# Two-part matrix products in mixers A and C: one wide product for the high weight part, its two sums joined on eviction

## The chip, the cores and the metric

One NeuronCore of a Trainium2 chip runs the whole program. The metric is the device time of one execution in microseconds; the median of several executions counts, and less is better. The profile is of one more execution of the same program.

## The reference

A trunk of four pre-RMSNorm residual layers over x (1, 256 tokens, 2048 features), float32, with mixers A, B, C, A and a final RMSNorm. Each layer does `x = x + mixer(rmsnorm(x))`.

- A is dilated sliding-window attention. `proj = h @ w_in` gives q, k and v of three groups (windows 128, 512, 2048 with dilations 1, 4, 16) with 8 heads of 128, and a gate of 1024 columns. q and k get a rotary on their first 32 dims; scores are scaled by 128^-0.5; the three groups' outputs are joined by a softmax over their log denominators; the result is multiplied by `silu(gate)` and goes through `w_out`.
- B is a convolution module: `val * sigmoid(glu)`, a depthwise convolution of 31 taps, LayerNorm, SiLU, a gate, and `w_out`.
- C is a retention in two chunks of 128 tokens with 8 heads (q, k of 256 dims with rotary, v of 512), a normalisation per head, `silu(gate)` and `w_out`.

Nearly all of the arithmetic lies in the products with the weight matrices, 391 MB of them, each read once.

## The kernel before, in words

x is held transposed: eight tiles `X[c]` of [128 features, 2, 256 tokens], and beside them `XHL[c]`, [128, 2, 2, 256], the normalised input in a high and a low part (L297, L303), so that a product of float32 quality is made of fp32r products: high weight by high x, high weight by low x, low weight by high x. The RMSNorm's per-token factor `rstd` is put in only when a result leaves PSUM.

Weights come as slabs of 1 MB, called pieces (`chunk_ws`, `chunk_xs`, `group_ws` list them all in order). The main loop (L1062) takes piece i: its products `p.mm`, then `cut(i + 2)`, which splits a later slab into `wh` (ScalarE copy, L1056) and `wl` (VectorE subtract, L1057; for some pieces of B on GpSimd) and issues the load of the slab after on SP (L1045); then `after`, the eviction of a finished chunk; then `pop`, which takes steps from the list `side` by their costs and a budget. A step pushed with `brk=True` ends that pop, and steps pushed by `after` wait for the next piece, since `avail` is counted before. `raw`, `wh` and `wl` have three buffers each. PSUM has 4 accumulator banks (`ps_acc`), 2 for scores (`ps_s`) and 2 for transposes (`ps_t`).

Three forms of products stand in the code. `mm_ws` (L138) keeps 128 weight columns in the array and streams 256 tokens: per k tile and 128 features the three products L154, L155 and L156, all into one half of a bank, so that a chunk of 256 features is one bank. A slab of 8 k tiles and 256 columns has 48 such products. `mm_xs` (L176) keeps x in the array and streams 512 weight columns (L188 to L190, 24 products a slab). `mm_xs2` (L159) does the same with 256 columns and is used in B alone.

In A (L354) six `chunk_xs` chunks give v; then, for each of four head pairs, six `chunk_ws` chunks of two slabs give q and k of the three groups. `after_qk` (L471) multiplies the bank by `rstd_p` (L475), shuffles 32 partitions (L477) and rotates them on GpSimd (L478 to L480). The last k of a head pair calls `attention(hp)` (L483), which pushes seven groups (L541), each of one step of `scores` (L488), `turn` and `values` for the four units of a head pair; the exponent is `A.activation(p, p, AF.Exp, bias=..., scale=128^-0.5)` (L504). Then four gate chunks follow (`after_gate`, L543), whose step `z` (L548) builds the input of the output projection, and in layer 0 eight output chunks of one slab each (L592), which `new_x` (L287) adds to X. In layer 3 the output projection is of the form `mm_xs`.

C (L885) has for each of eight heads a q and a k chunk of the form `mm_ws` (`after_qk`, L896: two multiplies from the bank, L902 and L903, and two adds), and v and gate chunks of the form `mm_xs`. After every second head an output projection over a quarter of the features runs, 8 chunks of one slab each, 32 in all (`outp`, L1008, with `new_x`).

`ScalarE` runs its instructions in the order in which they are issued, as do VectorE, GpSimd and the SP queue; the order above is thus each engine's own.

Of the kernel before, what the change touches and what calls it, by code (L numbers as in the profile page):

```python
# [54 lines left out]
def tile_hybrid_trunk(ctx: ExitStack, tc, x, positions, norm_w, final_norm_w, a_w_in, a_w_out,  # L55
# [82 lines left out]
    def mm_ws(np_, p, kts, hold, xs, nb=1):  # L138
# [18 lines left out]
        return f  # L157

    def mm_xs2(np_, p, kts, hold, xs):  # L159

        def f(wh, wl):
            if p == 0:
                hold["ps"] = [ps_acc()]
            kk = len(kts)
            for t in range(2):
                for i in range(kk):
                    ps = hold["ps"][0][:, t * 256:(t + 1) * 256]
                    xh, xl = (v[:, t * 128:(t + 1) * 128] for v in xs(kts[i]))
                    T.matmul(ps, xh, wh[:, i, :], start=p == 0 and t == 0 and i == 0, stop=False,  # L169
                             skip_group_check=True)  # L170
                    T.matmul(ps, xh, wl[:, i, :], start=False, stop=False, skip_group_check=True)  # L171
                    T.matmul(ps, xl, wh[:, i, :], start=False, stop=p == np_ - 1 and i == kk - 1,  # L172
                             skip_group_check=True)
        return f

    def mm_xs(np_, p, kts, hold, xs):  # L176

        def f(wh, wl):
            if p == 0:
                hold["ps"] = [ps_acc(), ps_acc()]  # L180
            kk = len(kts)
            order = [(i, t) for i in range(kk) for t in range(2)]
            if p == np_ - 1:
                order = [(i, t) for t in range(2) for i in range(kk)]
            for i, t in order:
                ps = hold["ps"][t]
                xh, xl = (v[:, t * 128:(t + 1) * 128] for v in xs(kts[i]))
                T.matmul(ps, xh, wh[:, i, :], start=p == 0 and i == 0, stop=False)  # L188
                T.matmul(ps, xh, wl[:, i, :], start=False, stop=False)  # L189
                T.matmul(ps, xl, wh[:, i, :], start=False, stop=p == np_ - 1 and i == kk - 1)  # L190
        return f

    def x_of(kt):
        return XHL[kt // 2][:, kt % 2, 0], XHL[kt // 2][:, kt % 2, 1]

# [5 lines left out]
    def chunk_ws(w, c0, nk, after, xs=x_of, kt0=0, before=None, lo=lambda p: "v", budget=3.0, hold=None,  # L201
                 mm=None):
        hold = {} if hold is None else hold
        mm = mm or mm_ws
        np_ = nk // 8
        for p in range(np_):
            kts = list(range(p * 8, p * 8 + 8))
            pieces.append(Piece(wslab(w, kt0 + p * 8, 8, c0, 256), 8, 256, mm(np_, p, kts, hold, xs),
                                after=(lambda: after(hold["ps"][0])) if p == np_ - 1 else None,
                                before=before if p == 0 else None, lo=lo(p), budget=budget))  # L210
# [76 lines left out]
    def new_x(c, ps, layer, perm):  # L287

        V.tensor_tensor(X[c], v3(ps), X[c], op=OP.add)
        if layer is None:  # L290
# [63 lines left out]
    def layer_a(L, wi, wo, first, next_layer, final):  # L354
# [116 lines left out]
        def after_qk(g, w, hp):  # L471
            def f(ps):
                q = lt([128, 2, S], F32, "qk", 8)
                QK[g, w, hp] = q
                V.tensor_tensor(q, v3(ps), row2(rstd_p), op=OP.mult)  # L475
                sw = tmp([128, 2, S])[:32]
# [6 lines left out]
        def attention(hp):  # L483
            units = [(h, qt) for h in range(2) for qt in range(2)]
            U = {}
            scale = 128.0 ** -0.5

            def scores(u):  # L488
# [6 lines left out]
                for g in (1, 2):  # L495
# [6 lines left out]
                                       stt[:, 0:1])  # L502
                V.tensor_scalar(stt[:, 1:2], stt[:, 0:1], -scale, None, op0=OP.mult)
                A.activation(p, p, AF.Exp, bias=stt[:, 1:2], scale=scale, accum_out=stt[:, 2:3])  # L504
                V.reciprocal(stt[:, 3:4], stt[:, 2:3])
# [12 lines left out]
            def values(u):  # L518
# [12 lines left out]
                A.activation(o[:, h, qt * 128:(qt + 1) * 128], ps, AF.Copy)  # L531

            for n in range(7):
                def group(n=n):
                    if n >= 3:
                        values(units[n - 3])
                    if 2 <= n < 6:
                        turn(units[n - 2])
                    if n < 4:
                        scores(units[n])  # L540
                push(2.9, group, brk=True)  # L541

        def after_gate(hp):  # L543
            def f(ps):
                g = lt([128, 2, S], F32, "g", 3)
                V.tensor_tensor(g, v3(ps), row2(rstd_p), op=OP.mult)

# [13 lines left out]

        s1, s2 = norm_stats(True, True)

# [23 lines left out]
        def z_of(kt):  # L587
            return ZT[kt // 2][:, kt % 2, 0], ZT[kt // 2][:, kt % 2, 1]

# [70 lines left out]
    def layer_b(L, wi, wo, next_layer):  # L660
# [4 lines left out]
        def tok(ps, t):  # L665
            return ps[t] if isinstance(ps, list) else ps[:, t * 256:(t + 1) * 256]

# [217 lines left out]
    def layer_c(L, wi, wo, next_layer):  # L885
# [10 lines left out]
        def after_qk(h, w):  # L896
            def f(ps):
# [3 lines left out]
                m2 = tmp([128, 2, S])  # L901
                V.tensor_tensor(m1, v3(ps), st["rope"][:, 0:1].to_broadcast([128, 2, S]), op=OP.mult)  # L902
                V.tensor_tensor(m2, v3(ps), st["rope"][:, 1:2].to_broadcast([128, 2, S]), op=OP.mult)  # L903
                V.tensor_tensor(o[:, 0], m1[:, 0], m2[:, 1], op=OP.subtract)
# [103 lines left out]
        def outp(p):  # L1008
            def z_of(kt):
                z = ZT[4 * p + kt // 2]  # L1010
                return z[:, kt % 2, 0], z[:, kt % 2, 1]
            need = 4 * p + 3
# [128 lines left out]
```

## Time and profile before

| | us |
|---|---|
| median of 3 executions | 2270.89 |
| lowest and highest | 2269.66 to 2271.91 |
| the profiled execution | 2272.37 |
| its span, first to last instruction | 2270.6 |
| mean granted TensorE clock | 0.991 |

The profiled execution's time is 1.8 us longer than its span. The profile has a page with the busy time of each engine, the chain of work that ended last and groups of instructions by line, and a trace that answers what each engine did when. PE is TensorE's matrix products, PEld its weight loads, DVE is VectorE, ACT ScalarE, POOL GpSimd and SP the queue that issues the loads. A product's duration in the trace runs through the array's pipeline, so that products overlap; the distance from one start to the next is what one costs.

### The profile page before, as it was taken

How to read it: one execution, taken by the hardware profiler on the slowest of the kernel's cores; microseconds unless marked ns; L12 is line 12 of the kernel's file. 1: busy time of each engine (PE TensorE's matmuls, PEld its weight loads, DVE VectorE, ACT ScalarE, POOL GpSimd, SP SyncE). 2: the span in 40 equal slices, each digit the busy share in tenths (PEclk: the TensorE clock that was granted, in tenths of full speed). 3: DMA queues.
4: the chain of work that ended last, by engine and by line, in shares of the span. 5: the costliest groups of instructions: out<-in, count | busy, mean ns of one | idle time of the engine just before them, and what ended most of it. 6: DMA issues, size and time to landing. Idle time of an engine off the chain costs nothing.

```text
span 2270.6 us, 34549 instructions
## 1 busy us (share of the span) xinstructions
PE 2227.4 (98%) x15024; PEld 2066.4 (91%) x15024; DVE 1333.5 (59%) x1537; ACT 976.0 (43%) x905; POOL 554.4 (24%) x273
## 2 busy tenths in 40 slices
PE   8999999999999997999999999999999999999998
PEld 7789999999998877989889889899988889999996
DVE  5545565556597886565555545455556446555554
ACT  4343433445444444444443444344355333333353
POOL 3005334321478972100000000000001015334311
PEclk9999999999999998999999999999999999999999
DMA  6555445446555553555555555555555555444444
GB/s 222 186 199 176 159 158 169 152 141 197 170 179 189 174 167 134 184 188 180 179 186 177 201 168 174 196 175 170 191 173 171 190 191 182 151 164 167 154 145 148
DMA packets 301424, 395.95 MB, mean 174 GB/s; under 512 B 6615, under 2 KB 212823, under 8 KB 301269
## 3 DMA queue, kind: packets, MB, share of 16 engines
q1 hardware_dynamic: 299280, 391.14, 51.9%
q8 instruction: 117, 1.92, 0.3%
q10 hardware_dynamic: 1592, 1.93, 0.3%
q0 software_dynamic: 400, 0.67, 0.1%
q14 instruction: 35, 0.28, 0.0%
HBM read 391.63 MB, written 2.10 MB: 173 GB/s over the span
## 4 chain that ended last, share of the span: by engine, by line
PE 92%; DVE 3%; POOL 2%; ACT 2%; issue 1%; DMA 0%; DVEq 0%; ACTq 0%
PE ps_acc L156 16%; PE ps_acc L155 16%; PE ps_acc L154 16%; PE ps_acc L189 11%; PE ps_acc L188 11%; PE ps_acc L190 11%; PE ps_acc L172 1%; PE ps_acc L171 1%; PE ps_acc L169 1%; PE ps_t L530 1%; POOL tmp L479 1%; DVE wl L1057 1%; PE ps_t L965 1%; PE ps_s L497 1%; ACT wh L1056 1%
## 5 line engine op out<-in xcount | busy, mean ns | idle before, releaser
L1057 DVE TENSOR_TENSOR wl<-raw,wh 128x2048 fp32r<-128x2048 f32 (+1 forms) x329 | 782.2, 2379 | 559.3 <-ACT wh L1056 557.2
L1056 ACT ACTIVATE wh<-raw 128x2048 fp32r<-128x2048 f32 (+1 forms) x371 | 703.4, 1898 | 713.3 <-PE ps_acc L155 333.9
L154 PE MATMUL ps_acc<-xhl,wh 128*128 128x256 f32 x2304 | 657.6, 285 | 0.0
L156 PE MATMUL ps_acc<-xhl,wl 128*128 128x256 f32 x2304 | 652.7, 283 | 0.0
L155 PE MATMUL ps_acc<-xhl,wh 128*128 128x256 f32 x2304 | 652.6, 283 | 0.1
L189 PE MATMUL ps_acc<-wl,xhl 128*128 128x512 f32 x1152 | 451.1, 392 | 3.0 <-DVE wl L1057 2.8
L188 PE MATMUL ps_acc<-wh,xhl 128*128 128x512 f32 x1152 | 453.8, 394 | 0.2 <-ACT wh L1056 0.2
L190 PE MATMUL ps_acc<-wh,xhl 128*128 128x512 f32 x1152 | 450.6, 391 | 0.0
L155 PEld LDWEIGHTS ps_acc<-xhl,wh 128*128 128x128 f32 x2304 | 442.5, 192 | 0.7 <-DVE xhl L303 0.3
L154 PEld LDWEIGHTS ps_acc<-xhl,wh 128*128 128x128 f32 x2304 | 442.5, 192 | 0.4
L156 PEld LDWEIGHTS ps_acc<-xhl,wl 128*128 128x128 f32 x2304 | 442.3, 192 | 0.0
L189 PEld LDWEIGHTS ps_acc<-wl,xhl 128*128 128x128 f32 x1152 | 217.7, 189 | 48.4 <-DVE wl L1057 4.4
L190 PEld LDWEIGHTS ps_acc<-wh,xhl 128*128 128x128 f32 x1152 | 217.4, 189 | 45.4
L188 PEld LDWEIGHTS ps_acc<-wh,xhl 128*128 128x128 f32 x1152 | 217.7, 189 | 44.9 <-ACT wh L1056 0.6
L478 POOL TENSOR_TENSOR qk<-qk,ropeA 32x512 f32<-32x512 f32 x48 | 63.6, 1325 | 611.6 <-DVE tmp L477 611.6
L1057 POOL TENSOR_TENSOR wl<-raw,wh 128x2048 fp32r<-128x2048 f32 x42 | 194.6, 4635 | 69.7 <-ACT wh L1056 54.2
L274 POOL COPY ssq<-tmp 128x512 f32<-128x512 f32 x4 | 5.6, 1411 | 830.0 <-ACT tmp L299 812.0
L154 PE MATMUL ps_acc<-z,wh 128*128 128x256 f32 x512 | 145.5, 284 | 0.0
L156 PE MATMUL ps_acc<-z,wl 128*128 128x256 f32 x512 | 145.2, 284 | 0.0
L155 PE MATMUL ps_acc<-z,wh 128*128 128x256 f32 x512 | 144.7, 283 | 0.0
L479 POOL TENSOR_TENSOR tmp<-tmp,ropeA 32x512 f32<-32x512 f32 x48 | 121.0, 2520 | 0.0
L722 DVE SCALAR_TENSOR_TENSOR ps_s<-u,bw,ps_s 128x256 f32<-128x256 f32 x232 | 91.8, 483 | 26.2 <-ACT ps_s L720 26.2
(224 smaller groups left out, 2610.5 us busy)
## 6 DMA issues: line engine op xcount, KB each, us to landing
raw<-in_a_w_in_dram SPq DMA_DIRECT2D x159, 1024.0 KB, 5.0
raw<-in_c_w_in_dram SPq DMA_DIRECT2D x96, 1024.0 KB, 5.0
raw<-in_b_w_in_dram SPq DMA_DIRECT2D x48, 1024.0 KB, 5.1
raw<-in_c_w_out_dram SPq DMA_DIRECT2D x32, 1024.0 KB, 5.7
raw<-in_a_w_out_dram SPq DMA_DIRECT2D x16, 1024.0 KB, 5.7
raw<-in_b_w_out_dram SPq DMA_DIRECT2D x16, 1024.0 KB, 5.0
xin<-in_x_dram SPq DMA_DIRECT2D x4, 512.0 KB, 8.7
out_dram<-qk SPq DMA_DIRECT2D x8, 256.0 KB, 2.6
```

Of the source, the lines that this page charges most:

```text
L154: T.matmul(ps, w_h, xh, start=st, stop=False, skip_group_check=True)
L155: T.matmul(ps, w_h, xl, start=False, stop=False, skip_group_check=True)
L156: T.matmul(ps, w_l, xh, start=False, stop=last and i == kk - 1, skip_group_check=True)
L169: T.matmul(ps, xh, wh[:, i, :], start=p == 0 and t == 0 and i == 0, stop=False, skip_group_check=True)
L188: T.matmul(ps, xh, wh[:, i, :], start=p == 0 and i == 0, stop=False)
L189: T.matmul(ps, xh, wl[:, i, :], start=False, stop=False)
L190: T.matmul(ps, xl, wh[:, i, :], start=False, stop=p == np_ - 1 and i == kk - 1)
L478: G.tensor_tensor(q[:32], q[:32], ropeA[:, 0:1].to_broadcast([32, 2, S]), op=OP.mult)
L479: G.tensor_tensor(sw, sw, ropeA[:, 1:2].to_broadcast([32, 2, S]), op=OP.mult)
L722: V.scalar_tensor_tensor(ct[:, j] if k == TAPS - 1 else acc[j], src, w, acc[j], op0=OP.mult, op1=OP.add)
L1056: A.activation(wh[:, sl], r[:, sl], AF.Copy)
L1057: (V if p.lo == "v" else G).tensor_tensor(wl[:, sl], r[:, sl], wh[:, sl].bitcast(F32), op=OP.subtract)
```

## The change

`chunk_ws` takes a new form of products, `mm_wj`, for A and C: a chunk has two banks, one per 128 features. The high weight part meets the high and the low part of x, which lie side by side in `XHL` (and in the `z` tiles), in one product of 512 columns; the low weight part meets the high x in one of 256 columns. The bank then holds two sums, which are joined on eviction: `joined` copies the second to SBUF on ScalarE and adds the first on VectorE, per bank; `new_x` adds both to X, one after the other. In A, q is no longer multiplied by `rstd_p`; the factor goes into the scale of the exponent, per query row (`qs_`, two small instructions behind the column form of rstd). An empty step with `brk=True` is pushed ahead of attention's seven groups. B keeps its forms; `mm_xs` and `mm_xs2` only fetch the two parts of x in another way.

```diff
+    def mm_wj(np_, p, kts, hold, xs):
+        def f(wh, wl):
+            if p == 0:
+                hold["ps"] = [ps_acc(), ps_acc()]
+            last = p == np_ - 1
+            kk = len(kts)
+            order = [(nt, i) for nt in range(2) for i in range(kk)]
+            if hold.get("kouter") and p == 0:
+                order = [(nt, i) for i in range(kk) for nt in range(2)]
+            for nt, i in order:
+                x2 = xs(kts[i])
+                ps = hold["ps"][nt]
+                w_h = wh[:, i, nt * 128:(nt + 1) * 128]
+                w_l = wl[:, i, nt * 128:(nt + 1) * 128]
+                T.matmul(ps, w_h, x2, start=p == 0 and i == 0, stop=False, skip_group_check=True)
+                T.matmul(ps[:, 0:S], w_l, x2[:, 0], start=False, stop=last and i == kk - 1,
+                         skip_group_check=True)
+        return f
+
+    def sums(ps):
+        return [(b[:, 0:S], b[:, S:2 * S]) for b in ps]
+
+    def joined(dst, ps):
+        for j, (a, b) in enumerate(sums(ps)):
+            A.activation(dst[:, j], b, AF.Copy)
+            V.tensor_tensor(dst[:, j], a, dst[:, j], op=OP.add)
...
     def x_of(kt):
-        return XHL[kt // 2][:, kt % 2, 0], XHL[kt // 2][:, kt % 2, 1]
+        return XHL[kt // 2][:, kt % 2]
...
     def chunk_ws(w, c0, nk, after, xs=x_of, kt0=0, before=None, lo=lambda p: "v", budget=3.0, hold=None,
...
-        mm = mm or mm_ws
+        mm = mm or mm_wj
...
-                                after=(lambda: after(hold["ps"][0])) if p == np_ - 1 else None,
+                                after=(lambda: after(hold["ps"])) if p == np_ - 1 else None,
...
     def new_x(c, ps, layer, perm):
-        V.tensor_tensor(X[c], v3(ps), X[c], op=OP.add)
+        if isinstance(ps, list):
+            for h in range(2):
+                for j, parts in enumerate(sums(ps)):
+                    V.tensor_tensor(X[c][:, j], parts[h], X[c][:, j], op=OP.add)
+        else:
+            V.tensor_tensor(X[c], v3(ps), X[c], op=OP.add)
...
                 QK[g, w, hp] = q
-                V.tensor_tensor(q, v3(ps), row2(rstd_p), op=OP.mult)
+                joined(q, ps)
+                if w == 1:
+                    V.tensor_tensor(q, q, row2(rstd_p), op=OP.mult)
...
-                V.tensor_scalar(stt[:, 1:2], stt[:, 0:1], -scale, None, op0=OP.mult)
-                A.activation(p, p, AF.Exp, bias=stt[:, 1:2], scale=scale, accum_out=stt[:, 2:3])
+                V.tensor_scalar(stt[:, 1:2], stt[:, 0:1], qs_[:, 2 + qt:3 + qt], None, op0=OP.mult)
+                A.activation(p, p, AF.Exp, bias=stt[:, 1:2], scale=qs_[:, qt:qt + 1], accum_out=stt[:, 2:3])
...
+            push(0.0, lambda: None, brk=True)
             for n in range(7):
                 def group(n=n):
...
         def after_gate(hp):
             def f(ps):
                 g = lt([128, 2, S], F32, "g", 3)
-                V.tensor_tensor(g, v3(ps), row2(rstd_p), op=OP.mult)
+                joined(g, ps)
+                V.tensor_tensor(g, g, row2(rstd_p), op=OP.mult)
...
+        def s2():
+            s2_()
+            qs_ = st["qs"] = lt([128, 4], F32, "qs")
+            V.tensor_scalar(qs_[:, 0:2], rcol, 128.0 ** -0.5, None, op0=OP.mult)
+            V.tensor_scalar(qs_[:, 2:4], rcol, -(128.0 ** -0.5), None, op0=OP.mult)
...
-                V.tensor_tensor(m1, v3(ps), st["rope"][:, 0:1].to_broadcast([128, 2, S]), op=OP.mult)
-                V.tensor_tensor(m2, v3(ps), st["rope"][:, 1:2].to_broadcast([128, 2, S]), op=OP.mult)
+                joined(m1, ps)
+                V.tensor_tensor(m2, m1, st["rope"][:, 1:2].to_broadcast([128, 2, S]), op=OP.mult)
+                V.tensor_tensor(m1, m1, st["rope"][:, 0:1].to_broadcast([128, 2, S]), op=OP.mult)
```

## Rows read from the trace of the kernel before

**Rows 1.** The page, busy us (share of the span) xinstructions of each engine.

```profile
PE 2227.4 (98%) x15024; PEld 2066.4 (91%) x15024; DVE 1333.5 (59%) x1537; ACT 976.0 (43%) x905; POOL 554.4 (24%) x273
```

**Rows 2.** The page, the chain that ended last, by engine.

```profile
PE 92%; DVE 3%; POOL 2%; ACT 2%; issue 1%; DMA 0%; DVEq 0%; ACTq 0%
```

**Rows 3.** Groups by form: out<-in, shapes xcount | busy us, mean ns | idle before.

```profile
L154 PE MATMUL ps_acc<-xhl,wh 128*128 128x256 f32 x2304 | 657.6, 285 | 0.0
...
L154 PE MATMUL ps_acc<-z,wh 128*128 128x256 f32 x512 | 145.5, 284 | 0.0
...
L154 PE MATMUL ps_acc<-v,wh 128*128 128x256 f32 x128 | 36.3, 283 | 0.0
```

**Rows 4.** Timeline of PE (start us, us), 256-column products, 18 steps apart.

```profile
399.81 0.28 PE L155 MATMUL ps_acc<-xhl,wh 128*128 128x256 f32 x1
...
401.97 0.28 PE L155 MATMUL ps_acc<-xhl,wh 128*128 128x256 f32 x1
```

**Rows 5.** Timeline of PE, 512-column products, 14 steps apart.

```profile
149.69 0.39 PE L190 MATMUL ps_acc<-wh,xhl 128*128 128x512 f32 x1
...
152.86 0.39 PE L189 MATMUL ps_acc<-wl,xhl 128*128 128x512 f32 x1
```

**Rows 6.** Stretches of 100 us: busy by engine, then granted clock, DMA share, GB/s.

```profile
100.00:200.00 100.00, 100.00 (x591) 89.32 (x591) 49.80 (x31) 36.56 (x21) 13.28 (x8) 1.00 0.57 190
...
400.00:500.00 100.00, 98.88 (x820) 98.32 (x820) 58.31 (x70) 41.43 (x41) 31.30 (x18) 1.00 0.45 148
```

**Rows 7.** Timeline of PE, a 256-column product followed by a 512-column one.

```profile
989.23 0.28 PE L156 MATMUL ps_acc<-xhl,wl 128*128 128x256 f32 x1
989.35 0.40 PE L188 MATMUL ps_acc<-wh,xhl 128*128 128x512 f32 x1
```

**Rows 8.** Timeline of PE, a 512-column product followed by a 256-column one.

```profile
161.93 0.39 PE L190 MATMUL ps_acc<-wh,xhl 128*128 128x512 f32 x1
162.15 0.28 PE L154 MATMUL ps_acc<-xhl,wh 128*128 128x256 f32 x1
```

**Rows 9.** Timeline of PE, first scores of a head pair, slab behind.

```profile
237.03 0.60 PE L494 MATMUL ps_s<-qk 128*128 128x256 f32 x2
...
239.22 0.36 PE L154 MATMUL ps_acc<-xhl,wh 128*128 128x256 f32 x1
```

**Rows 10.** Timeline of PE, second scores of that head pair, slab behind.

```profile
245.05 0.60 PE L494 MATMUL ps_s<-qk 128*128 128x256 f32 x2
...
245.84 0.36 PE L154 MATMUL ps_acc<-xhl,wh 128*128 128x256 f32 x1
```

**Rows 11.** Waits of PE: line <- releaser: us in total, times, longest.

```profile
PE ps_s L497 <- POOL qk L480: 9.0, 8, 1.1
```

**Rows 12.** Timeline of all engines, eviction and rotary of the last k.

```profile
231.47 0.69 DVE L475 TENSOR_TENSOR qk<-ps_acc,rstd_p 128x512 f32<-128x512 f32 x1 [1.64 <-PE ps_acc L156]
...
234.27 3.32 POOL L479 TENSOR_TENSOR tmp<-tmp,ropeA 32x512 f32<-32x512 f32 x1
...
237.66 1.25 POOL L480 TENSOR_TENSOR qk<-qk,tmp 32x512 f32<-32x512 f32 x1
```

**Rows 13.** Groups by form: VectorE and ScalarE reading 256 columns of a bank.

```profile
L617 DVE TENSOR_TENSOR qk<-ps_acc,x 128x256 f32<-128x256 f32 x16 | 5.9, 418 | 8.4 <-PE ps_acc L190 8.4
...
L680 ACT ACTIVATE sg<-ps_acc,rcol 128x256 f32<-128x256 f32 x8 | 3.4, 470 | 13.5 <-PE ps_acc L172 11.0 <-DVE rcol L269 2.6
```

**Rows 14.** Timeline of DVE, a residual add in C's output projection [idle before].

```profile
1689.84 0.69 DVE L289 TENSOR_TENSOR x<-ps_acc,x 128x512 f32<-128x512 f32 x1 [1.59 <-PE ps_acc L156]
```

**Rows 15.** Timeline of all engines, start of layer 0's output projection.

```profile
528.81 0.69 DVE L558 TENSOR_TENSOR v<-tmp,v 128x512 fp32r<-128x512 f32 x1 [0.70 <-ACT v L557]
...
529.85 0.28 PE L155 MATMUL ps_acc<-v,wh 128*128 128x256 f32 x1
```

**Rows 16.** DMA issues: KB each, median us to landing.

```profile
raw<-in_a_w_in_dram SPq DMA_DIRECT2D x159, 1024.0 KB, 5.0
```

More of the change, by code (lines that the diff above doesn't have):

```diff
@@ L167, in f @@
                     ps = hold["ps"][0][:, t * 256:(t + 1) * 256]
-                    xh, xl = (v[:, t * 128:(t + 1) * 128] for v in xs(kts[i]))
+                    xh, xl = (xs(kts[i])[:, h, t * 128:(t + 1) * 128] for h in range(2))
                     T.matmul(ps, xh, wh[:, i, :], start=p == 0 and t == 0 and i == 0, stop=False,
@@ L186, in f @@
                 ps = hold["ps"][t]
-                xh, xl = (v[:, t * 128:(t + 1) * 128] for v in xs(kts[i]))
+                xh, xl = (xs(kts[i])[:, h, t * 128:(t + 1) * 128] for h in range(2))
                 T.matmul(ps, xh, wh[:, i, :], start=p == 0 and i == 0, stop=False)
@@ L485, in attention @@
             U = {}
-            scale = 128.0 ** -0.5
+            qs_ = st["qs"]
             def scores(u):
@@ L560, in after_gate @@
             return f
-        s1, s2 = norm_stats(True, True)
+        s1, s2_ = norm_stats(True, True)
+        def s2():
[3 more added lines that the diff above has]
+            V.tensor_scalar(qs_[:, 2:4], rcol, -(128.0 ** -0.5), None, op0=OP.mult)
         n0 = len(pieces)
@@ L587, in z_of @@
         def z_of(kt):
-            return ZT[kt // 2][:, kt % 2, 0], ZT[kt // 2][:, kt % 2, 1]
+            return ZT[kt // 2][:, kt % 2]
         if not final:
@@ L665, in tok @@
         def tok(ps, t):
-            return ps[t] if isinstance(ps, list) else ps[:, t * 256:(t + 1) * 256]
+            return ps[t] if len(ps) == 2 else ps[0][:, t * 256:(t + 1) * 256]
         def turn(src, dst, bank=ps_acc):
@@ L1010, in z_of @@
                 z = ZT[4 * p + kt // 2]
-                return z[:, kt % 2, 0], z[:, kt % 2, 1]
+                return z[:, kt % 2]
             need = 4 * p + 3
```

## The prediction

> **What bounds the kernel now.** I read first the busy shares of the engines. The reader sees TensorE (PE) busy for 98% of the span and VectorE (DVE) for 59% [rows 1]. Then the chain of work that ended last: 92% of it is PE [rows 2]. So PE's products set the time, and a change pays by what it takes off PE's own line, or loses by what it makes PE wait for.
>
> Next the groups by form, to count the products that the change touches. The three products of `mm_ws` (L154 to L156) run 2304 times each against `xhl` (the input projections of mixers A and C), 512 times against `z` (C's output projection) and 128 against `v` (the output projection of layer 0's A) [rows 3]. B's output projection, against `big`, keeps `mm_ws`. So 2304 + 512 + 128 = 2944 triples become pairs.
>
> The busy time of these rows is no price: 284 to 285 ns each includes a pipeline that overlaps. The price is the distance from start to start, in the timeline. For 256 columns, 18 steps take 401.97 - 399.81 = 2.16 us: 0.120 us each [rows 4]. For 512 columns, 14 steps take 152.86 - 149.69 = 3.17 us: 0.2264 us each [rows 5]. The granted clock is 1.00 in the windows around both [rows 6], that is 2.4 GHz, at which 256 columns stream in 0.1067 us and 512 in 0.2133 us. So each product costs its columns and about 0.0133 us more, at either width. That fixed part is what the change can save.
>
> **The change, part by part.**
>
> Products. A triple of 256 columns costs 3 x 0.120 = 0.360 us. The pair has the same 768 columns in two products: 0.2266 + 0.120 = 0.3466 us, taking 0.0133 over the columns for the wide one. Each pair so saves 0.0133 us; 2944 x 0.0133 = 39.2 us. A mixed sequence does not stand in the trace, but its two steps do: a 256-column product followed by a 512-column one starts it 0.12 us later [rows 7], and a 512-column one followed by a 256-column one 0.22 us later [rows 8]. Neither order pays a surcharge, and neither gives more than the steady pace. From the steady rows the bounds are 2944 x 0.0124 = 36.5 us (0.2276 for the wide product, a nanosecond above) and 2944 x 0.0136 = 40.0 us (0.2264).
>
> On the same point the Trainium skill, "TensorE: Matmul & The Clock Gate", section "Back-to-back issue gap", gives a warm gap of N/2.4 + 2.5 ns. By it a triple would be 327.5 ns, a pair 325.0 ns, and the saving 2944 x 2.5 ns = 7.4 us (an estimate from that page); the rows show 13.3 ns, not 2.5, and the rows decide.
>
> Attention one slab later. Before, the first scores of each head pair came one slab behind the last k projection and waited for its rotary part on GpSimd (POOL). From the first product of the scores to the next slab's first product took 239.22 - 237.03 = 2.19 us [rows 9]; the second group of the same four products took 245.84 - 245.05 = 0.79 us [rows 10]. So 1.40 us is lost per head pair. The list of waits has it 8 times, four head pairs in two layers [rows 11]: 8 x 1.40 = 11.2 us. Is it gone? k is taken off at 231.47 and POOL ends it at 237.66 + 1.25 = 238.91 [rows 12]: 7.4 us. The new eviction is longer: ScalarE (ACT) copies 0.47 [rows 13], then the second copy and two adds of 0.42, of which one hides beside the copy, and the 0.69 multiply: 0.47 + 0.42 + 0.42 + 0.69 = 2.0 us in place of 0.69, so 1.3 us more, 8.7 us in all. Two slabs are now 2 x 16 x 0.3466 = 11.1 us. 2.4 us are left, so I take all 11.2 off. The bounds are 11.2 and 0.
>
> The empty step pushed ahead of attention issues nothing on any engine, so every queue (SP's loads, POOL's rotary work, DVE, ACT) only sees the seven groups behind one more slab's split. What is queued behind the scores on PE is the next slab, which no longer stands still. Scaling q in the exponent instead of in the eviction drops 24 multiplies on DVE, off the chain; the two small scale columns per layer are 4 tiny instructions. I cost both at nothing, under cover of DVE's 41% of idle time; without the cover the multiplies' loss would be a gain, and the four, at most 0.42 us each, would cost 1.7 us.
>
> Evictions. A bank now holds the high and low sums side by side. Each chunk of q, k or gate adds two ACT copies (0.47 each) and replaces one DVE operation by two of 0.42 and up to two more. It lies beside the next slab's products, since four accumulator banks hold two chunks. In the output projections the residual add becomes four of 0.42 = 1.67 us, in place of 0.69: 1.0 us more. In the steady slab there DVE idles 1.59 us [rows 14] of every 48 x 0.120 = 5.76 us; the slab shrinks to 5.55, so 1.59 - 1.0 - 0.2 = 0.4 us stays idle. Hidden, but nearly used up. If it were not, the price is the overrun per slab: at 0.69 an add (the whole-bank price, upper bound) 2.76 - 0.69 = 2.07 us more, 0.7 us over per slab, 40 such slabs, 28 us. I take nothing, since the 0.42 row has the same shape and the same kind of operands.
>
> Loads. A slab of 1 MB lands 5.0 us after its issue at the median [rows 16]; it must come every 5.55 us, three are in flight, and the 512-column stretches already run a slab in 24 x 0.2266 = 5.44 us. No cost.
>
> Start of layer 0's output projection. The last gate's z now meets both x parts in the first product. The seventh k tile comes 36 products after the start, 36 x 0.120 = 4.3 us; before, the low part was done at 528.81 + 0.69 = 529.50, and its first reader started at 529.85 [rows 15]. The eviction adds 1.3 us, the pairs bring the reader 0.2 us + 0.12 us forward, and the last attention group in front pushes it back by some 0.5 us: 0.35 - 1.3 - 0.3 + 0.5 = a stall of 0.8 us, once. Layer 3 needs that tile a slab later and pays nothing. Bounds: 0 and 2 us.
>
> Sum. The profiled execution took 2272.37 us, 1.5 above the median of the runs shown. 2272.4 - 39.2 - 11.2 + 0.8 = 2222.8; less that 1.5, and rounded up a little for small waits: **2222 us**.
>
> **The rivals.**
>
> (A) The wait for scores stays. The rotary chain grows beyond two slabs, or the first scores find DVE still at the split. For it: POOL's middle step took 3.32 us in the chain where the next one, of the same shape, took 1.25 [rows 12], so it can stretch. Against it: 2.4 us of room. Time: 2222 + 11.2 = 2233.
>
> (B) Products cost by columns alone. Then pair and triple are equal, the fixed part only moves into the wider product, and attention alone pays: 2222 + 39.2 = 2261. For it: no row shows the pair in a run of its own. Against it: the two widths' own paces and both changes of width [rows 4, 5, 7, 8]. By the gap that the Trainium skill's page "TensorE: Matmul & The Clock Gate" gives (section "Back-to-back issue gap") it would be 2222 + 39.2 - 7.4 = 2254, an estimate, and the trace does not agree with that gap: 0.120 us where it has 0.109.
>
> (C) Slower: the banks. A chunk now holds two of the four banks; in the 40 one-slab chunks of the output projections the chunk after next waits on PE until all four adds are done. It decides when the adds end over 5.55 us behind the chunk's last product. To end slower than before, the 49.6 us must be lost in 40 chunks, 1.24 us each; at 1.5 us each the time is 2222 + 60 = 2282. For it: DVE's 0.4 us of room [rows 14]. Against it: even the upper price of the adds gives 28 us.
>
> (D) Evictions eat part of it: 0.3 us in each of 40 slabs, or as much at the gates, 12 us: 2234.
>
> **How the numbers follow.** Forecast 0.74, A 0.08, D 0.09, B 0.05, C 0.03, no visible effect 0.01. The range reaches from 2217 (40.0 and 11.2 saved, no stall, and a run at the low end of the shown ones) to 2240 (A or D with the low bound of the product saving); it leaves out B, C and A together with D. A measurement of this kernel can tell about 0.2%, 4.5 us, from no change. All but C and the last case are faster by far more: faster 0.95, same 0.02, slower 0.03.
>
> **What would show it.** Right: in the timeline of a k projection, a 512-column product every 0.347 us with a 256-column one 0.227 us behind it; slabs 5.55 us apart; the wait of L497 for POOL gone from PE's list; the residual adds of about 0.42 us, four a chunk, with a remnant of idle time before them. Wrong: a pair pace near 0.360 (B); the scores' wait still listed (A); PE waiting in the accumulators' products for the adds or for DVE's low split (C, D). PE's busy share should stay near 98%, with 2944 fewer products and as many fewer weight loads.

## The result and the profile after

The changed kernel takes 2245.83 us, the median of 4 runs (2243.90 to 2248.17), beside 2270.98 us for the kernel before: a ratio of 0.989 (95% interval 0.9878 to 0.9903; later ratios have theirs in brackets). That is 25.1 us faster where 49 were forecast, and 5.8 us above the top of the range. The profiled execution is the slowest of the four, 2248.17 us with a span of 2246.4 us, against 2272.37 before.

The page of the kernel after: busy time of each engine, then the chain that ended last by engine, then two of its groups.

```profile
PE 2201.7 (98%) x12080; PEld 1907.3 (85%) x12080; DVE 1397.0 (62%) x1781; ACT 1028.5 (46%) x1049; POOL 555.7 (25%) x273
...
PE 91%; DVE 4%; ACT 3%; issue 1%; POOL 0%; DMA 0%; DVEq 0%; ACTq 0%
...
L175 PE MATMUL ps_acc<-xhl,wh 128*128 128x512 f32 x2304 | 817.1, 399 | 0.2 <-DVE xhl L338 0.2
L176 PE MATMUL ps_acc<-xhl,wl 128*128 128x256 f32 x2304 | 644.5, 280 | 0.0
```

PE is still the bound, at 98% [rows 1, 2], and the three products L154 to L156, of which [rows 3] shows the first, have become a wide one (L175) and a narrow one (L176). Two other views tell where the time went. First PE's list of waits of the kernel after (line, releaser, us in total, times, longest):

```profile
PE ps_t L567 <- ACT tmp L552: 8.7, 4, 3.0
...
PE ps_acc L219 <- DVE wl L1104: 2.8, 2, 1.8
```

The head of the list before, the scores' wait for GpSimd [rows 11], is gone. A new one stands in its place, not foreseen: the products of the probabilities with the values (L567) wait for ScalarE's copy of the transposed probabilities out of their bank (L552), 4 times, 8.7 us.

Second, PE's timeline of the kernel after (start, us; in brackets PE's idle time before the instruction and what ended it), in stretches: pairs in two different slabs, the first scores of a head pair, the values' products beside layer 0's gates and one beside layer 3's, and layer 3's output projection.

```profile
199.68 0.40 PE L175 MATMUL ps_acc<-xhl,wh 128*128 128x512 f32 x1
199.91 0.28 PE L176 MATMUL ps_acc<-xhl,wl 128*128 128x256 f32 x1
200.03 0.40 PE L175 MATMUL ps_acc<-xhl,wh 128*128 128x512 f32 x1
...
201.44 0.40 PE L175 MATMUL ps_acc<-xhl,wh 128*128 128x512 f32 x1
...
241.37 0.59 PE L531 MATMUL ps_s<-qk 128*128 128x256 f32 x2
241.79 0.61 PE L534 MATMUL ps_s<-qk 128*128 128x128 f32 x4
242.16 0.48 PE L175 MATMUL ps_acc<-xhl,wh 128*128 128x512 f32 x1
...
359.78 0.40 PE L175 MATMUL ps_acc<-xhl,wh 128*128 128x512 f32 x1
...
361.52 0.39 PE L175 MATMUL ps_acc<-xhl,wh 128*128 128x512 f32 x1
...
489.88 1.16 PE L567 MATMUL ps_t<-tmp,v 128*128 128x128 f32 x8 [1.44 <-ACT tmp L552]
...
507.86 1.16 PE L567 MATMUL ps_t<-tmp,v 128*128 128x128 f32 x8 [2.88 <-ACT tmp L552]
...
2183.40 1.16 PE L567 MATMUL ps_t<-tmp,v 128*128 128x128 f32 x8 [2.96 <-ACT tmp L552]
...
2191.61 0.40 PE L219 MATMUL ps_acc<-wl,v 128*128 128x512 f32 x1
...
2193.01 0.40 PE L219 MATMUL ps_acc<-wl,v 128*128 128x512 f32 x1
```

Five pairs take 201.44 - 199.68 = 1.76 us, 0.352 each, in the first stretch, and 361.52 - 359.78 = 1.74, 0.348 each, in the other slab. Over all pairs that stand next to each other in the trace at a granted clock of 1.00 the wide product takes 233.6 ns and the narrow one 117.0 from start to start: 350.6 ns, where the prediction had 346.7. The scores now hold PE for 242.16 - 241.37 = 0.79 us, as the second group did before [rows 10], and not 2.19 [rows 9]. At layer 0's gates PE stands still for 1.44 and 2.88 us, at layer 3's for 2.96. (The last two lines are read with e10.)

Where ScalarE was meanwhile is in its own timeline, kernel after, in front of the first of these two waits:

```profile
483.10 0.63 ACT L186 ACTIVATE g<-ps_acc 128x256 f32<-128x256 f32 x2
483.74 1.28 ACT L588 ACT_TABLE_LOAD   x1
486.94 0.63 ACT L588 ACTIVATE g<-g 128x512 f32<-128x512 f32 x1 [1.92 <-DVE g L585]
488.71 0.63 ACT L596 ACTIVATE v<-tmp 128x512 fp32r<-128x512 f32 x1 [1.14 <-DVE tmp L591]
489.25 0.58 ACT L552 ACTIVATE tmp<-ps_t 128x512 f32<-128x512 f32 x1
```

The transposes (L550) were issued at 481.4. Their copy (L552) came at 489.25, behind the whole of the gate's step z: silu with its table load (L588), then the product with the output and z's high part (L596). Twice in it ScalarE itself waits for VectorE (1.92 and 1.14 us) with the copy queued behind it.

### The profile page after: what moved, and what is told of

It reads as the page before. It is cut to its first block, busy times and chain, and to the rows that moved or that the text cites. A ratio compares the mean times of both kernels' runs of the same rounds, so it can differ in the third digit from the quotient of the medians.

```text
span 2246.4 us, 29151 instructions
## 1 busy us (share of the span) xinstructions
PE 2201.7 (98%) x12080; PEld 1907.3 (85%) x12080; DVE 1397.0 (62%) x1781; ACT 1028.5 (46%) x1049; POOL 555.7 (25%) x273
## 4 chain that ended last, share of the span: by engine, by line
PE 91%; DVE 4%; ACT 3%; issue 1%; POOL 0%; DMA 0%; DVEq 0%; ACTq 0%
PE ps_acc L175 29%; PE ps_acc L176 15%; PE ps_acc L218 12%; PE ps_acc L219 12%; PE ps_acc L220 12%; DVE wl L1104 2%; PE ps_acc L199 1%; PE ps_acc L202 1%; PE ps_acc L201 1%; ACT wh L1103 1%; PE ps_acc L156 1%; PE ps_acc L154 1%; PE ps_acc L155 1%; PE ps_t L567 1%; PE ps_t L1012 1%
## 5 line engine op out<-in xcount | busy, mean ns | idle before, releaser
L175 PE MATMUL ps_acc<-xhl,wh 128*128 128x512 f32 x2304 | 817.1, 399 | 0.2 <-DVE xhl L338 0.2
L176 PE MATMUL ps_acc<-xhl,wl 128*128 128x256 f32 x2304 | 644.5, 280 | 0.0
L175 PEld LDWEIGHTS ps_acc<-xhl,wh 128*128 128x128 f32 x2304 | 433.3, 188 | 101.9 <-DVE xhl L338 0.6
L219 PE MATMUL ps_acc<-wl,xhl 128*128 128x512 f32 x1152 | 450.8, 391 | 2.8 <-DVE wl L1104 2.8
L176 PEld LDWEIGHTS ps_acc<-xhl,wl 128*128 128x128 f32 x2304 | 435.2, 189 | 0.4
L219 PEld LDWEIGHTS ps_acc<-wl,xhl 128*128 128x128 f32 x1152 | 217.6, 189 | 48.5 <-DVE wl L1104 4.3
L515 POOL TENSOR_TENSOR qk<-qk,ropeA 32x512 f32<-32x512 f32 x48 | 85.0, 1772 | 590.6 <-DVE tmp L514 590.6
L175 PE MATMUL ps_acc<-z,wh 128*128 128x512 f32 x512 | 180.8, 395 | 0.0
L176 PE MATMUL ps_acc<-z,wl 128*128 128x256 f32 x512 | 144.6, 283 | 0.0
L175 PEld LDWEIGHTS ps_acc<-z,wh 128*128 128x128 f32 x512 | 96.2, 188 | 21.8
L516 POOL TENSOR_TENSOR tmp<-tmp,ropeA 32x512 f32<-32x512 f32 x48 | 102.6, 2138 | 0.0
L768 DVE SCALAR_TENSOR_TENSOR ps_t<-u,bw,ps_t 128x256 f32<-128x256 f32 x232 | 91.9, 483 | 11.1 <-ACT ps_t L766 11.1
L176 PEld LDWEIGHTS ps_acc<-z,wl 128*128 128x128 f32 x512 | 96.3, 188 | 0.2
```

Of the source, the lines that this page charges most:

```text
L175: T.matmul(ps, w_h, x2, start=p == 0 and i == 0, stop=False, skip_group_check=True)
L176: T.matmul(ps[:, 0:S], w_l, x2[:, 0], start=False, stop=last and i == kk - 1, skip_group_check=True)
L515: G.tensor_tensor(q[:32], q[:32], ropeA[:, 0:1].to_broadcast([32, 2, S]), op=OP.mult)
L516: G.tensor_tensor(sw, sw, ropeA[:, 1:2].to_broadcast([32, 2, S]), op=OP.mult)
L768: V.scalar_tensor_tensor(ct[:, j] if k == TAPS - 1 else acc[j], src, w, acc[j], op0=OP.mult, op1=OP.add)
```

## The experiments

My theory after reading the two traces has two halves. The widths: alternating them costs time itself, so that a pair saves 9.4 ns and not 13.3; the rival is that PE loses that time elsewhere, in evictions and waits. The queue: the empty step moved attention's groups beside the gates, and z stands in front of the copy on ScalarE there; the rival is that the longer evictions of the gate make the wait, and the empty step has no part in it.

**e1_triples: the wide product as two narrow ones.** All the rest of the change stays.

```diff
-                T.matmul(ps, w_h, x2, start=p == 0 and i == 0, ...)
+                T.matmul(ps[:, 0:S], w_h, x2[:, 0], start=p == 0 and i == 0, ...)
+                T.matmul(ps[:, S:2 * S], w_h, x2[:, 1], start=False, ...)
```

> The changed kernel with the wide product taken apart again: three products of 256 columns per pair, same banks, evictions and attention order. If the pair is worth what the trace of the changed kernel shows (350.6 ns on the mean in place of 360), this costs 2944 x 9.4 ns = 27.7 us: 2273 us, and the products stand 0.120 us apart throughout. If the pair were worth the forecast 13.3 ns, 2285; if only 2.5 ns, 2253.

Measured: 2273.27 us (2271.39 to 2275.71), ratio 1.0011 [1.0002, 1.0021] to before. PE's timeline of e1 is back at 0.120 us a product: (400.49 - 399.53) / 8.

```profile
399.53 0.28 PE L176 MATMUL ps_acc<-xhl,wh 128*128 128x256 f32 x1
...
400.49 0.28 PE L175 MATMUL ps_acc<-xhl,wh 128*128 128x256 f32 x1
```

The pair alone is worth 2273.27 - 2245.83 = 27.4 us, 9.3 ns for each of 2944. And all of the rest together, attention's 11 us included, is worth nothing (+2 us): in e1's list of waits the scores' wait is gone and the values' stands at 7.1 us.

**e2_runs8: fewer changes of width.** Eight wide products, then the eight narrow ones that belong to them.

```diff
-            for nt, i in order:
-                T.matmul(ps, w_h, x2, ...)
-                T.matmul(ps[:, 0:S], w_l, x2[:, 0], ...)
+            for j in range(0, len(order), run):
+                for nt, i in order[j:j + run]:
+                    T.matmul(hold["ps"][nt], wh[...], xs(kts[i]), ...)
+                for nt, i in order[j:j + run]:
+                    T.matmul(hold["ps"][nt][:, 0:S], wl[...], xs(kts[i])[:, 0], ...)
```

> The changed kernel with the same products in another order: per 128 features of a slab the eight wide ones, then the eight narrow ones. Theory: it is the alternation of widths that costs 350.6 ns a pair where runs of one width cost 226.7 + 120.0 = 346.7; then 2944 x 3.9 ns = 11.5 us less, 2234 us, and all products stand 227 or 120 ns apart. Rival: the wide product with the two parts of x costs more by itself; then 2246, and the wide ones stay 233 ns apart.

Measured: 2244.63 us (2241.97 to 2248.75), ratio 0.9886 [0.9869, 0.9902], not to be told from the change as it was. PE's timeline of e2 (the runs grouped):

```profile
201.24 2.00 PE L173 MATMUL ps_acc<-xhl,wh 128*128 128x512 f32 x8
203.08 1.11 PE L176 MATMUL ps_acc<-xhl,wl 128*128 128x256 f32 x8
204.03 2.00 PE L173 MATMUL ps_acc<-xhl,wh 128*128 128x512 f32 x8
```

Eight and eight take 204.03 - 201.24 = 2.79 us, 349 ns a pair, with one change of width in eight products, where the alternation has one at every product. So the price is not paid per change alone. Single steps in such a run show how: behind the change the wide products stand 233, 236, 229, 232 and 231 ns apart, and only then 226 to 227. The new width has a tail of five products, and a run of eight holds all of it. The theory was right about the size and wrong about its form: it had this kernel 10 us faster. The time is the rival's (2246), its sign is not: the wide ones do not stay at 233 ns. Over all its pairs e2 takes 349.5 ns, which is 3.2 us less than the change; its profiled execution, the slowest of the four, lost about as much to the granted clock, which stood at 0.50 from 506.5 to 513.0 and from 2182.5 to 2185.8, behind both layers' long values' waits (some 5 us lost, where the change's execution lost 1.7).

The trace of before had shown that tail. These are the lines behind [rows 7], of PE's timeline of the kernel before, where B's first 512-column products follow:

```profile
989.58 0.40 PE L189 MATMUL ps_acc<-wl,xhl 128*128 128x512 f32 x1
...
990.51 0.39 PE L190 MATMUL ps_acc<-wh,xhl 128*128 128x512 f32 x1
990.73 0.39 PE L188 MATMUL ps_acc<-wh,xhl 128*128 128x512 f32 x1
```

From the first at 989.35 [rows 7] the five steps to 990.51 take 1.16 us, 0.232 each, and the next 0.22.

**e3_no_step: the pairs without the empty step.**

```diff
-            push(0.0, lambda: None, brk=True)
```

> The changed kernel without the empty step ahead of attention. Theory: the scores' wait for the rotary on GpSimd is back and longer than before, since the eviction of k is longer by 1.3 to 2 us and the slab shorter by 0.15: 2.9 to 3.5 us in each of 8 head pairs, 23 to 28 us; the wait of the values' products for the copy of the transposed weights (some 11 us with the clock's fall) is gone: 2257 to 2263 us. Rival: that wait comes from the longer gate eviction and not from attention's place; then it stays and the time is 2268 or more.

Measured: 2264.16 us (2263.87 to 2269.96), ratio 0.9976 [0.9965, 0.9988]. PE's list of waits of e3:

```profile
PE ps_s L534 <- POOL qk L517: 16.6, 8, 2.1
PE ps_t L567 <- ACT tmp L552: 3.5, 2, 1.8
```

The scores' wait is back, and longer than before the change (16.6 us against 9.0 [rows 11]): the new eviction ends k later, and the slabs are shorter. Taken by itself the empty step is worth 2264.2 - 2245.8 = 18 us to this kernel, more than the 11.2 that the kernel before had to give. The two profiled executions are 16.7 us apart, and their traces account for it: 18.8 us more at the scores from start to start, 5.3 less at the values, and the granted clock at 0.50 behind three waits in place of one, 3.4 us more. And without the step the values' wait falls from four times to two and from 8.7 to 3.5 us, where the theory had it gone. The kernel before, with attention at the same place, has no such wait in its list, so the rival has a part: what the change does beside the step, the longer eviction of the gate above all, makes 3.5 us by itself. No run has the step without the longer eviction, so what the step would make alone is open.

**e4_step_not_last: no empty step for the last head pair,** the one whose groups fall beside the gates.

```diff
-            push(0.0, lambda: None, brk=True)
+            if hp < 3:
+                push(0.0, lambda: None, brk=True)
```

> The empty step for the first three head pairs of a layer only; the last one, whose attention runs beside the gate chunks, starts where it did before. Theory: the values' wait (some 11 us) goes, the scores' wait is back for 2 of 8 head pairs (2.9 to 3.5 us each): 2245.8 - 11 + 6.5 = 2241 us. Rival (the gate eviction alone makes the wait): 2252.

Measured: 2246.01 us (2242.61 to 2246.40), ratio 0.9887 [0.9872, 0.9902]: 5 us above the forecast and no better than the change. The values' wait shrank to 0.9 us in the list (1.7 from start to start), but the scores' wait is there for the last pair of each layer. From PE's list of waits of e4:

```profile
PE ps_s L534 <- POOL qk L517: 4.2, 2, 2.1
```

and behind one of them, of 2.10 us and over at 2139.60, PE runs slower. The windows of e4: stretch, its length, busy time of PE, weight loads, DVE, ACT and POOL, then PE's granted clock, DMA share and GB/s:

```profile
2136.00:2140.00 4.00, 1.90 (x13) 1.57 (x12) 0.00 (x0) 0.00 (x0) 3.47 (x3) 0.99 0.74 251
2140.00:2144.00 4.00, 4.00 (x16) 3.44 (x16) 1.65 (x6) 2.71 (x3) 0.00 (x0) 0.58 0.03 11
```

So where attention stands does make the values' wait, but moving it back trades one wait for another.

**e5_z_behind: z one place further back,** behind the first group of attention that follows, so that the copy comes first on ScalarE.

```diff
-                push(1.5, z, front=hp < 3)
+                if hp < 3:
+                    side.insert(1, (1.5, z, False, None))
+                else:
+                    push(1.5, z)
```

> The changed kernel with the gate's step z put behind the next attention group in the list instead of in front of it, so that ScalarE copies the transposed weights before it turns to the gate. Theory: the wait of the values' products (9.5 us from start to start over both layers, and about 1 us for the clock's fall behind it) is made by ScalarE's order of work in the gate slabs; it goes: 2245.8 - 10.5 = 2235 us. Rival: the longer gate eviction holds up ScalarE and VectorE anyway; then at least half of the wait stays and the time is 2241 or more.

Measured: 2236.29 us (2235.83 to 2237.43), ratio 0.9848 [0.9833, 0.9862], 9.5 us below the change and 1.3 above the forecast. ScalarE's timeline of e5 at the same place:

```profile
480.32 0.63 ACT L186 ACTIVATE g<-ps_acc 128x256 f32<-128x256 f32 x2
480.85 0.60 ACT L552 ACTIVATE tmp<-ps_t 128x512 f32<-128x512 f32 x1
...
487.82 1.28 ACT L588 ACT_TABLE_LOAD   x1
```

The copy now follows the gate's own eviction at once; z's table load starts 7.5 us behind that eviction's start in place of 0.6; and L567 is out of PE's list. In its place that list has the stall at the start of layer 0's output projection that the prediction expected:

```profile
PE ps_acc L175 <- DVE v L597: 1.2, 1, 1.2
```

This settles the queue: the wait hangs on the order of two steps on ScalarE. The longer gate evictions are still there in e5, and with the copy in front nothing waits for them but that once.

**e6_runs2: two wide, two narrow** (e2 with a run of 2). It asks whether the price goes by the number of changes, half as many here as in the change.

> The changed kernel with runs of two: two wide products, then two narrow ones. Theory: each change from narrow to wide starts the same sequence, of which the runs of eight show the steps (wide ones 6, 9, 2, 5 and 4 ns over 227, then none; the first narrow one 6 to 7 under 120). Runs of two then cut it after 6 + 9 ns: 15 - 7 = 8 ns per two pairs, a pair at 350.7 ns, no better than alternating (350.6). Rival: the price is one fixed sum per change (3.9 ns a pair when alternating); then half of it per pair, 348.6 ns.

One execution: 2242.80 us, beside 2267.33 for the kernel before on the same chip (one as well), 24.5 us less: by its time it is not to be told from the change, and the price of a pair is read from its trace. PE's timeline of e6:

```profile
199.94 0.63 PE L173 MATMUL ps_acc<-xhl,wh 128*128 128x512 f32 x2
...
202.03 0.62 PE L173 MATMUL ps_acc<-xhl,wh 128*128 128x512 f32 x2
```

Six pairs in 202.03 - 199.94 = 2.09 us: 348.3 ns, and 348.5 over the whole trace, the number of the rival. The wide ones stand 233 apart throughout, so the tail never ends; the narrow ones take 112 to 119, less than their steady 120. A short narrow run so gives back part of what the wide one pays. Why it does is open.

**e8_flip: runs of 32.** A slab's 16 wide and 16 narrow products in two runs, the order turned round in every second slab.

```diff
+            runs = ["h", "l"] if turns[0] % 2 == 0 else ["l", "h"]
+            steps = [(part, nt, i) for part in runs for nt, i in order]
...
+                if part == "h":
+                    T.matmul(ps, w, x2, ...)
+                else:
+                    T.matmul(ps[:, 0:S], w, x2[:, 0], ...)
```

> The changed kernel with each slab's 32 products ordered by width, sixteen wide and sixteen narrow, every second slab the other way round, so that runs of 32 of one width follow each other. Theory: the price is that of the change from narrow to wide, some 22 us per thousand changes as in the runs of eight (2796 against 2773 ns a run); with one such change per 32 pairs a pair costs 347.4 ns in place of 350.6: 2944 x 3.2 = 9.4 us less, 2236 us. Rival: the wide products against both parts of x cost more by themselves; then a pair stays at 349 to 350 and the time at 2243 to 2246.

Measured: 2242.83 us (2240.76 to 2244.61), ratio 0.9875 [0.9861, 0.989], 3 us below the change and 7 above the forecast. PE's timeline of e8:

```profile
361.39 4.00 PE L186 MATMUL ps_acc<-xhl,wl 128*128 128x256 f32 x32
365.22 7.44 PE L184 MATMUL ps_acc<-xhl,wh 128*128 128x512 f32 x32
372.50 0.76 PE L186 MATMUL ps_acc<-xhl,wl 128*128 128x256 f32 x5
```

32 and 32 take 372.50 - 361.39 = 11.11 us, 347.2 ns a pair: the tail is paid once in 32, and against x the forecast's 346.7 is nearly reached (347.7 over all pairs against x). The mean over all pairs is 348.3, since the wide products against `z`, C's output projection, keep 232.6 ns even in runs of this length. The profiled execution also lost the clock behind layer 3's long values' wait (0.50 from 2178.6 to 2181.9), where the change's did not: 1.7 us.

**e9_flip_z: e8 and e5 together.**

> Both of the two others together. If the two shortfalls are separate, the gains add: 2245.8 - 10.5 - 9.4 = 2226 us, PE's busy line without the values' wait and a pair at 347.4 ns. If they share a cause, less.

Measured: 2230.10 us (2229.29 to 2230.51), ratio 0.9819 [0.9802, 0.9835]. The two gains (3.0 and 9.5 us) should give 2233.3; they give 3 us more than that, 4 less than the forecast. Part of the 3 us is that second fall of the clock in e8: e9 has neither the values' waits nor a fall behind them.

**e10_qs_32 and e11_flip_z_pad: where the operands lie.** The wide products against `z`, and layer 3's output projection, whose code the change does not touch, both run slower than 227 ns a step. In the last stretch of the timeline of after, layer 3's, six steps take 2193.01 - 2191.61 = 1.40 us, that is 233 ns each; before, these products stood 226.8 apart. 192 of them make 1.2 us. What the change does near them is a small tile of 16 bytes per partition for the scale of the scores, `qs`, allocated ahead. The theory: such a tile moves the big tiles behind it to addresses at which the 512-column reads are slower. e10 widens that tile to 128 bytes; e11 is e9 with four such tiles (`st`, `qs`, `vm`, `ro`) at 128 bytes.

```diff
-            qs_ = st["qs"] = lt([128, 4], F32, "qs")
+            qs_ = st["qs"] = lt([128, 32], F32, "qs")
```

> The changed kernel with its small scale tile made 32 columns wide (128 bytes a partition) in place of 4 (16 bytes); nothing else. Of layer 3's output projection, whose code the change does not touch, the 512-column products stand 233 ns apart in the changed kernel and 227 before. Theory: the tile of 16 bytes, there allocated ahead of the tiles of z, moves them off an alignment that the reads like; then these 192 products are back at 227 ns, 1.2 us in all. Rival: they are slower because of what precedes them or of other traffic; then 233 ns stays.

One execution: 2250.22 us, layer 3's output at 232.4 ns a step. The theory fell for that place.

> The version with runs of 32 of one width and z behind the group, with all small tiles of the scopes (16 bytes) made 128 bytes wide. Theory as for the run beside it: the wide products against C's z (232.7 ns in runs of one width, where those against x take 228.0) fall to 228, 512 x 4.7 = 2.4 us, and layer 3's output projection gives 1.2 us: 2230 - 3.6 = 2226.5 us. Rival: z's products are slower for another reason; then 2229 to 2230.

Measured: 2227.99 us (2227.42 to 2229.78), ratio 0.9809 [0.9795, 0.9822]. Two timelines of PE at C's output projection, first e9's, then e11's:

```profile
1181.68 3.19 PE L184 MATMUL ps_acc<-z,wh 128*128 128x512 f32 x13
1184.70 2.06 PE L186 MATMUL ps_acc<-z,wl 128*128 128x256 f32 x16
```

```profile
1180.71 5.60 PE L184 MATMUL ps_acc<-z,wh 128*128 128x512 f32 x24
1186.15 2.08 PE L186 MATMUL ps_acc<-z,wl 128*128 128x256 f32 x16
```

13 wide products take 1184.70 - 1181.68 = 3.02 us, 232 ns each, in e9, and 24 take 5.44, 227 each, in e11. For C's `z` the padding does what was expected (232.7 to 228.0 over all 512 of them, 2.4 us); layer 3's products stay at 232.4, and the time lies 1.5 us above the forecast. That the sizes of the small tiles matter is shown for the one place, since nothing else differs; that they act through the addresses of the big tiles is the likely reading, but no run shows an address, and what slows layer 3 stays open. This version, 43.8 us below the kernel before on its chip, is the fastest of the study.

## Why the prediction was wrong

**What bounds the kernel.** Right: PE at 98% throughout, and every gain and loss above is one of PE's line.

**The products: the step that failed first.** The prediction worked out 346.7 ns a pair from two steady paces, and checked the mixed sequence with the one step across each change of width: "Neither order pays a surcharge" [rows 7, 8]. The step across the change is indeed unpaid. The surcharge is in the steps behind it: five wide products at 232 instead of 227 ns, which in an alternation never end. The narrow ones give back 3 ns (117.0 against 120.0), the wide ones pay 7 (233.6 against 226.6): 3.9 ns a pair, 2944 x 3.9 = 11.5 us of the 39.2. So the term is 27.7 us by the trace and 27.4 by e1, below the prediction's own low bound of 36.5. By the gap on the Trainium skill's page "TensorE: Matmul & The Clock Gate" (section "Back-to-back issue gap"), which gives it for a single product, the pair would take 325 ns and save 2.5 (an estimate from the page); it takes 350.6 and saves 9.4. Rival B had the right place, but not the size: the pair saves two thirds of the forecast, not nothing.

**Attention one slab later.** Right for the scores: 0.79 us a head pair in place of 2.19, and 10.6 us less from start to start over all attention products, against 11.2 forecast. The room of 2.4 us was enough; rival A fell. e3 shows that the reasoning about the longer eviction was needed: without the step the wait would have grown to 16.6 us.

**The empty step: the step that failed second.** That every queue "only sees the seven groups behind one more slab's split" was costed at nothing. But groups of attention stand in one list with steps of other owners, and z is pushed to the front of that list behind each slab that ends a gate chunk. ScalarE then does z, and its two waits for VectorE, ahead of the copy that PE needs one slab later. For the last head pair this was so in the kernel before already, for the transposes of the fourth group, and it just fitted. ScalarE's timeline of the kernel before, z's table load and the copy:

```profile
497.70 1.28 ACT L549 ACT_TABLE_LOAD   x1
...
503.22 0.59 ACT L515 ACTIVATE tmp<-ps_t 128x512 f32<-128x512 f32 x1
```

The copy came 5.7 us behind its transposes (497.53) and ended at 503.81, 0.8 us before PE's next products of the values (504.59). In the kernel after it comes 7.8 us behind them (489.25 - 481.41), and PE is ready 1.44 us before it can go on. The delay puts the transposes of the third and the fifth group there in place of the fourth and the sixth, and without it (e3) the fourth alone waits, 1.8 us in layer 0. So the prediction missed two things: that 0.8 us was all the room there, and that the step changes which groups need it. In PE's list it is 8.7 us; from start to start 9.4. And behind layer 0's long wait, 2.88 us, PE runs on slowly. The windows of the kernel after, with the same columns as e4's above; the last stretch lies behind layer 3's wait of 2.96 us, over at 2183.40:

```profile
504.60:507.90 3.30, 0.42 (x4) 0.10 (x2) 1.89 (x4) 2.00 (x5) 0.00 (x0) 1.00 0.96 303
507.90:511.60 3.70, 3.70 (x19) 3.41 (x20) 1.96 (x1) 3.58 (x4) 0.00 (x0) 0.64 0.02 4
511.60:515.30 3.70, 3.70 (x21) 3.23 (x21) 2.96 (x3) 1.08 (x2) 0.00 (x0) 0.89 0.55 163
...
2183.00:2187.00 4.00, 3.60 (x25) 3.33 (x26) 2.24 (x2) 4.00 (x5) 0.00 (x0) 1.00 0.08 30
```

At 0.64 in place of 1.00 the second stretch does 2.4 us of work in 3.7, 1.3 us lost, and the third another 0.4 (from 509 to 512 the clock is 0.50, that is 1.2 GHz of 2.4); behind layer 3's wait nothing is lost. Waits and clock come to 9.4 + 1.7 = 11.1 us. e5, which changes that order alone, gains 9.5 net of its own stall of 1.2: 10.7. Rival D had "as much at the gates, 12 us", by evictions alone; that its size came near is luck, since the order on ScalarE is not in it.

**Evictions and the residual adds.** Right for the banks; the gate's eviction has the part in the values' wait that e3 shows. The groups by form of the kernel after:

```profile
L322 DVE TENSOR_TENSOR x<-ps_acc,x 128x256 f32<-128x256 f32 x160 | 59.5, 418 | 26.1 <-PE ps_acc L176 26.0
...
L186 ACT ACTIVATE qk<-ps_acc 128x256 f32<-128x256 f32 x96 | 36.7, 382 | 130.5 <-PE ps_acc L176 130.5
```

An add takes 418 ns as taken from [rows 13], and VectorE still waits for PE before the residual adds (26.0 us in 40 chunks, 0.65 each where 0.4 was forecast). The copies take 382 ns where 470 were taken. No accumulator product waits for them: rival C fell.

**Loads.** Right: no DMA among PE's waits but that at the start, and L219's wait for VectorE is 2.8 us as it was before.

**Start of layer 0's output projection.** A stall of 0.8 us was forecast. It does not stand in the list after, and with the values' waits gone it appears at 1.2 us (e5), where z also comes later. The term was right in kind; that the values' waits hid it, by letting z get ahead, is my reading and not shown apart.

**Layer 3's output projection** was not in the prediction at all, since its code stays: 1.2 us, of a cause that is open.

**Sum.** 11.5 for the pairs, 11.1 for the values' waits and the clock, 1.2 for layer 3 and 0.6 less won at the scores make 24.4, less the 0.8 of the stall that did not come: 23.6 us. They are read from the profiled execution, which took 2248.17 us where the prediction's sum for one, before it took off 1.5, was 2222.8: 25.4 us more. The other 1.8 us lie in many small differences and are not told apart. Either of the two large terms alone would have stayed in the range; it left out the two together. Its ends do not come out of the terms that it names (those give 2218.5 and 2236.7), but the result lies outside both. A together with D, by their prices, would come to 2245 us, the measured time; that is luck, since the scores' wait of A is gone.

## What to carry to other kernels

A steady pace of each shape is no price for a mixed sequence: look in the trace at the five or six steps behind a change, not only at the step across it. A step that only delays others moves them into the neighbourhood of other steps: list, for each queue, what stands in front of each moved instruction in its new slab, above all steps that are pushed to the front. Where a copy is all that PE waits for, let it go ahead of a chain that itself waits for a second engine.

## What was not expected of the hardware

Behind a change from 256 to 512 columns the wide products took 233, 236, 229, 232 and 231 ns before they came to 227, and the first narrow ones behind a wide one 112 to 119 before 120, all at a granted clock of 1.00. Against x alone a pair took 350.4 ns in the alternation, 348.4 in runs of 2, 349.1 in runs of 8 and 347.7 in runs of 32. Over the steady 346.7 that is about 4, 3, 19 and 32 ns for each change of width and back; why short runs are cheap is open.

The granted clock fell behind a wait of 2.88 us (0.64 over the next 3.7 us) and one of 2.10 us (0.58 over the next 4.0, in e4), PE having run at 0.99 to 1.00 up to both, so that a wait cost more than the list of waits shows; behind one of 2.96 us it stayed at 1.00. The wait in the same place, 3.0 us long, was followed by 0.50 in e2, e6 and e8; and of e3's eight scores' waits of about 2 us each, two were followed by 0.50 and six by 1.00. Why is open. So one execution can be 1.7 us and more longer than another by the clock behind a wait alone.

512-column products against one tile took 232.7 ns, and 228.0 when only the sizes of four small tiles were changed (e11): the size of a small tile can slow products that have nothing to do with it.
